# One group of gates in classical form behind the neighbourhood attention, features summed on VectorE, and modulation spread from global attention to w_out

## The chip, the cores and the metric

The kernel runs on one core of one Trainium2 chip. The core's engines run side by side, each with its own stream of instructions: TensorE (PE in the profile; PEld is its loading of stationary operands), VectorE (DVE), ScalarE (ACT), GpSimd (POOL) and SyncE (SP, which here only starts DMA transfers). The metric is the device time of one execution in microseconds, the median of several executions of one program.

## The reference

One encoder block on 512 tokens with a model width of 2048, all in float32:

```python
mod = silu(c) @ w_ada + b_ada                  # 2048 x 12288
sh1, sc1, g1, sh2, sc2, g2 = split(mod, 6)
h = rms_norm(x, norm1_w) * (1 + sc1) + sh1
qa, ka, va, qb, kb, vb, ga, gb = split(h @ w_in)
ya = global_gqa(rope(rms_norm(qa)), rope(rms_norm(ka)), va)     # 8 heads, 2 key-value heads
yb = neighbourhood_attention(qb, kb, vb, rpb)                   # 8 heads, windows of 8 x 16
m  = sigmoid(ga) * (ya @ w_oa) + sigmoid(gb) * (yb @ w_ob)
x  = x + g1 * (m @ w_out)
h2 = rms_norm(x, norm2_w) * (1 + sc2) + sh2
x  = x + g2 * ((silu(h2 @ w_gate) * (h2 @ w_up)) @ w_down)
out = rms_norm(x, final_w)
```

ga and gb are each 512 x 2048. Only sh1 and sc1 are needed at the start. The other four rows of mod (g1, sh2, sc2, g2) are first needed at the end of `w_out` and later: this is what the text calls modulation.

## The kernel before

**Float32 from two halves.** Every operand of a matmul is split into a high part (ScalarE, L167) and a low part (VectorE, L169), and each product is three matmuls: high by high, high by low, low by high (L187, L188, L189). A *unit* of weights is one 128x1024 block: one DMA of 0.5 MB on SP's queue into a buffer `raw`, one split on ScalarE and one on VectorE into `whl`, and then its products. There are four buffers `raw` and three `whl`, and one to three more in some stages.

**Classical and seven-product groups.** `form1` and `form2` compute a column group directly: a unit gives 24 products of 128x512 (a product being one of the three matmuls). `group7` computes 512 columns by seven half-size products in place of eight: VectorE first forms sums of weight blocks (`wforms`), and a group takes 336 matmuls of 128x256 where the classical form takes 192 of 128x512. The same trick needs sums of the features h: `whole_features` adds the high and low parts of a feature back together (L908, 16 additions of 128x512 on GpSimd), and `feature_forms` forms the sums from that (L918 to L921, VectorE) and splits them.

**The stages that the change touches, in order.** (1) The second half of the global queries, global attention, and the classical gates GA 12 to 15 and GB 0 to 3. (2) The groups by seven products: gates GB 4 to 15 in three groups (`gates7(1)` to `gates7(3)`) and the neighbourhood values in two. (3) Neighbourhood attention ("attention B"): four pairs of heads, each with classical queries and keys, then scores S, a softmax over ScalarE and VectorE, transposes into the bank T (L1008), and products into Y. (4) `w_oa`, (5) `w_ob`, both classical, with the gates, which were kept in DRAM, loaded again and multiplied in, and (6) `w_out`, classical, with the first residual. After these come the feed-forward groups, which the change leaves alone.

**Modulation as filler.** The late part of mod is 128 units. A unit is one DMA of 0.5 MB into a buffer `mw` (three of them, L351), and one VectorE operation of 128x1024 that multiplies it by a scalar of silu(c) and adds it to a sum `acc` (L373). 16 units make one group; then the sum is split, multiplied by a matrix of ones on TensorE (L390), copied out (L394) and kept in DRAM. `slot()` is called twice in each weight unit and once in each half of a head: it adds `pace["rate"]` to an account `due` and starts one step of modulation when the account has reached 1. `later` is a list of things to do, one per unit; `soon` holds what is due in some units' time. Before the change, 96 units run from the start of attention B through `w_oa` to the first five pairs of columns of `w_ob`, with their DMAs on GpSimd's queue, and 32 in `w_out`, with their DMAs on SP's queue. The loads of the residual's x and of the first gate's rows (`rows(gate, g1_d)`, on GpSimd's queue) are made through `later` in `w_out`'s first units. At the last pair of heads of attention B the eight results of global attention are loaded and split at once (`attended`).

**What sets the order.** The program is written stage by stage, and a scheduler of the framework then orders each engine's instructions by its own estimate of when operands are ready. So a step that is written behind another can come between its instructions, where its operands and buffers allow it. The tile pools set which buffers share memory: a pool that is released before another is allocated makes the second wait for the first.

## Time and profile before

| | |
|---|---|
| runs of the kernel | 2526.19, 2533.56, 2535.54 us (median 2533.56) |
| the profiled execution | 2529.71 us, of which the profile's span is 2527.9 us |
| mean granted clock of TensorE | 0.991 |
| TensorE busy | 2448.4 us, 97% of the span, 17327 matmuls |
| VectorE busy | 2022.3 us, 80% |
| ScalarE busy | 1073.6 us, 42% |
| GpSimd busy | 169.8 us, 7% |
| moved by DMA | 461.78 MB, mean 183 GB/s |

In the profiled execution the stages lie as follows, in microseconds from the start of the span. TensorE's first products of a stage and the last ones of the stage before can mix, so the bounds are those of its main part.

| stage | from | to |
|---|---|---|
| queries, global attention, gates GA 12 to 15 and GB 0 to 3 | 230 | 456 |
| groups by seven products | 456 | 640 |
| attention B | 640 | 859 |
| w_oa | 859 | 958.7 |
| w_ob | 958.7 | 1050.3 |
| w_out | 1050.3 | 1240 |

Rows of the profile read thus. A row of the view of windows gives, for a stretch of time, its length, then for each engine the busy time and, in brackets, the number of instructions; then the clock that TensorE was granted (1.00 is full speed), the share of time in which the DMA engines were busy, and what they moved. A row of waits gives an engine, its bank or tile and line, behind the arrow what it waited for, and then the total, the number of waits and the longest one. A row of a timeline gives an instruction's start and duration, and in square brackets the idle time ahead of it and what ended it.

### The profile page before, as it was taken

Reading aid. Unit: us, or ns where it says so; the run is one execution under the profiler, and the core shown is the slowest. Engines: PE = TensorE matmul, PEld = TensorE weight load, DVE = VectorE, ACT = ScalarE, POOL = GpSimd, SP = SyncE. Lnnn points to the kernel's source line nnn. Section 1 sums busy time; section 2 is a strip of 40 time slices with the busy share of each in tenths; the row PEclk is TensorE's granted clock in tenths of the full one; section 3 lists DMA queues with packets and bytes.
Section 4 is the critical chain, followed back from the end, with each engine's and each line's share of the span. In section 5 each row is a group of like instructions: output and inputs, shape, how many; then the busy total and the mean of one; then the engine's idle time right before and its main releaser. Section 6 shows DMA issues by size and latency. Waiting matters only on the chain.

```text
span 2527.9 us, 42439 instructions
## 1 busy us (share of the span) xinstructions
PE 2448.4 (97%) x17327; PEld 2285.7 (90%) x17327; DVE 2022.3 (80%) x2690; ACT 1073.6 (42%) x1470; POOL 169.8 (7%) x254
## 2 busy tenths in 40 slices
PE   8999998999999899999999999999999999999998
PEld 7888887999877678878999999999999998999997
DVE  8985877987688778558798888888888885778877
ACT  5223554444334433224764444444444454434333
POOL 0100002100012221002000000000000000000010
PEclk9999999999999999999999999999999999999999
DMA  9865232444687798588544434434444456647563
GB/s 352 312 230 164 61 102 74 130 130 142 209 269 264 263 317 281 167 303 294 164 126 134 134 119 138 129 110 134 127 132 134 127 162 225 205 142 250 186 236 129
DMA packets 213732, 461.78 MB, mean 183 GB/s; under 512 B 15152, under 2 KB 59552, under 8 KB 204832
## 3 DMA queue, kind: packets, MB, share of 16 engines
q1 hardware_dynamic: 176608, 318.68, 39.1%
q0 software_dynamic: 27424, 123.81, 14.1%
q10 hardware_dynamic: 9504, 16.58, 1.8%
q8 instruction: 136, 2.23, 0.4%
q14 instruction: 60, 0.49, 0.1%
HBM read 412.84 MB, written 46.17 MB: 182 GB/s over the span
## 4 chain that ended last, share of the span: by engine, by line
PE 65%; DVE 13%; issue 9%; DMA 9%; ACT 2%; POOL 1%; DVEq 0%; POOLq 0%; SPq 0%; ACTq 0%
PE mm L189 13%; PE mm L187 13%; PE mm L188 13%; PE S L187 5%; PE S L189 5%; PE S L188 5%; DMA mw<-in_ada_w 4%; DVE whl L169 3%; DMA raw<-in_w_down 3%; PE Y L187 2%; PE Y L188 2%; PE Y L189 2%; DVE raw L508 2%; DVE acc L373 1%; DMA yr<-y 1%
## 5 line engine op out<-in xcount | busy, mean ns | idle before, releaser
L167 ACT ACTIVATE whl<-raw 128x1024 fp32r<-128x1024 f32 (+1 forms) x483 | 453.6, 942 | 666.0 <-PE mm L189 253.5
L169 DVE TENSOR_TENSOR whl<-raw,whl 128x1024 fp32r<-128x1024 f32 (+1 forms) x483 | 519.7, 1087 | 133.4 <-ACT whl L167 132.8
L169 DVE TENSOR_TENSOR whl<-ta,whl 128x1024 fp32r<-128x1024 f32 x124 | 151.6, 1223 | 78.6 <-ACT whl L167 78.6
L167 ACT ACTIVATE whl<-tb 128x1024 fp32r<-128x1024 f32 x124 | 131.5, 1061 | 183.8 <-PE S L189 121.8
L167 ACT ACTIVATE whl<-ta 128x1024 fp32r<-128x1024 f32 x124 | 131.3, 1059 | 170.6 <-PE mm L189 110.6
L373 DVE SCALAR_TENSOR_TENSOR acc<-mw,cact,acc 128x1024 f32<-128x1024 f32 x124 | 158.6, 1279 | 37.6 <-DMA mw<-in_ada_w 36.8
L169 DVE TENSOR_TENSOR whl<-tb,whl 128x1024 fp32r<-128x1024 f32 x124 | 151.3, 1220 | 8.6 <-ACT whl L167 7.1
L679 DVE TENSOR_TENSOR ta<-raw,ta 128x512 f32<-128x512 f32 x124 | 86.4, 697 | 33.7 <-DMA raw<-in_w_down 27.8
L678 DVE TENSOR_TENSOR ta<-raw 128x512 f32<-128x512 f32 x124 | 85.5, 690 | 32.1 <-DMA raw<-in_w_down 29.5
L187 PE MATMUL mm<-x56h,whl 128*128 128x256 f32 x336 | 92.4, 275 | 0.0
L188 PE MATMUL mm<-x56l,whl 128*128 128x256 f32 x336 | 92.4, 275 | 0.0
L189 PE MATMUL mm<-x56h,whl 128*128 128x256 f32 x336 | 92.4, 275 | 0.0
L187 PE MATMUL mm<-whl,s 128*128 128x256 f32 x320 | 88.1, 275 | 0.0
L680 DVE TENSOR_TENSOR tb<-raw 128x512 f32<-128x512 f32 x124 | 86.3, 696 | 2.1 <-DMA raw<-in_w_down 0.2
L187 PE MATMUL mm<-x3h,whl 128*128 128x256 f32 x320 | 88.0, 275 | 0.0
L188 PE MATMUL mm<-x3l,whl 128*128 128x256 f32 x320 | 88.0, 275 | 0.0
L189 PE MATMUL mm<-x3h,whl 128*128 128x256 f32 x320 | 88.0, 275 | 0.0
L187 PE MATMUL S<-x56h,whl 128*128 128x256 f32 x320 | 88.0, 275 | 0.0
L188 PE MATMUL S<-x56l,whl 128*128 128x256 f32 x320 | 88.0, 275 | 0.0
L189 PE MATMUL S<-x56h,whl 128*128 128x256 f32 x320 | 88.0, 275 | 0.0
L188 PE MATMUL mm<-whl,s 128*128 128x256 f32 x320 | 88.0, 275 | 0.0
L189 PE MATMUL mm<-whl,s 128*128 128x256 f32 x320 | 88.0, 275 | 0.0
(1837 smaller groups left out, 8929.2 us busy)
## 6 DMA issues: line engine op xcount, KB each, us to landing
raw<-in_w_in SPq DMA_DIRECT2D x133, 512.0 KB, 4.5
mw<-in_ada_w POOLq DMA_DIRECT2D x96, 512.0 KB, 5.4
raw<-in_w_gate SPq DMA_DIRECT2D x92, 512.0 KB, 3.9
raw<-in_w_up SPq DMA_DIRECT2D x88, 512.0 KB, 3.8
raw<-in_w_down SPq DMA_DIRECT2D x88, 512.0 KB, 5.2
raw<-in_ada_w POOLq DMA_DIRECT2D x29, 1024.0 KB, 7.2
raw<-in_w_out SPq DMA_DIRECT2D x48, 512.0 KB, 5.5
mw<-in_ada_w SPq DMA_DIRECT2D x32, 512.0 KB, 4.8
```

Of the source, the lines that this page charges most:

```text
L167: high = pin(S.activation(hi, src, AF.Copy))
L169: latest[:] = [high, pin(eng.tensor_sub(lo, src, hi))]
L187: nc.tensor.matmul(o, lh, rh, start=start, stop=False, **kw)
L188: nc.tensor.matmul(o, lh, rl, start=False, stop=False, **kw)
L189: nc.tensor.matmul(o, ll, rh, start=False, stop=stop, **kw)
L373: behind(V.scalar_tensor_tensor(acc, part, cact[:, k:k + 1], acc, op0=ALU.mult, op1=ALU.add))
L508: V.scalar_tensor_tensor(raw, raw, 1.0, call, op0=ALU.mult, op1=ALU.mult, accum_out=y)
L678: V.tensor_sub(t1, b12, b11)
L679: V.tensor_sub(t2_, b22, t1)
L680: V.tensor_sub(t3, b22, b12)
```

## The change

- `slot()` caps its account at 1.5. A new `finish()` drains all units of modulation that are left up to the current limit, sets the rate to 0 and then does what is still due.
- Modulation's first group (16 units) runs from the second half of the global queries through global attention, at a rate of 0.45, in a pool of its own with one sum, and is drained behind the gates GA 12 to 15. 64 units run in attention B at 0.55, on through the moved gates and `w_oa`, and are drained behind `w_oa`. The last 48 run in `w_ob` at 0.7 and in `w_out` at 0.6 and then 0.35, and are drained ahead of the first half of the norm. Their DMAs go to GpSimd's queue up to the end of `w_ob`.
- The gates GB 4 to 7 are not computed by a group of seven products but classically, behind attention B. In that stretch the results of global attention are loaded, one in each unit; those of neighbourhood attention are loaded from the fourth unit of `w_oa`, through buffers `raw`.
- `whole_features` adds on VectorE and no longer on GpSimd.
- `w_ob` has no additional buffers any more (before: one `raw` and two `whl`).
- The load of the first gate's rows moves from ahead of the load of x's first quarter to ahead of its second.

```diff
--- before.py
+++ after.py
@@ -212,7 +212,7 @@
     pace = {"rate": 0.0, "due": 0.0}
 
     def slot():
-        pace["due"] += pace["rate"]
+        pace["due"] = min(pace["due"] + pace["rate"], 1.5)
         if pace["due"] >= 1 and (fetched or mod["next"] < mod["end"]):
             pace["due"] -= 1
             advance(mods)
@@ -226,6 +226,12 @@
             later.pop(0)()
         advance(bg)
         slot()
+
+    def finish():
+        while fetched or mod["next"] < mod["end"]:
+            advance(mods)
+        pace["rate"] = 0.0
+        flush()
 
     def flush():
         while bg or soon:
@@ -360,7 +366,7 @@
 
     def ada_acc(bias, done):
 
-        acc = mod["pool"].tile([P, 1024], F32, tag="acc", name="acc", bufs=2)
+        acc = mod["pool"].tile([P, 1024], F32, tag="acc", name="acc", bufs=mod["accs"])
         if bias is not None:
             G.memset(acc, 0.0)
             nc.gpsimd.dma_start(acc[0:1, :], b_ada[:, bias:bias + 1024])
@@ -826,6 +832,10 @@
     q = pair(p_a, "q", 4 * T, 1)
     bg.extend([normed(kv, 2, nw["k"], kT), normed(q_acc, 4, nw["q"], q), values()])
     q1 = [st(F32) for _ in range(NT)]
+    p_w = tc.alloc_tile_pool(name="p_w0", bufs=1, side="right")
+    mod.update(pool=p_w, end=16, accs=1)
+    mods.append(ada_mod(0, (s2, b_sc2, n2, t2, b_sh2)))
+    pace["rate"] = 0.45
     form2(w_in, QA + 512, hT, lambda i, b: S.activation(q1[i], b, AF.Copy))
     flush()
 
@@ -879,9 +889,10 @@
     q = pair(p_a, "q", 4 * T, 1)
     bg.append(normed(q1, 4, nw["q"], q))
     gates(sg_a, GA, 12, 16)
-    flush()
+    finish()
     for h in range(4):
         att_a(4 + h, q, h, 1)
+    p_w.release()
     p_a.release()
     p_q.release()
     p_o = []
@@ -905,7 +916,7 @@
         f = (p_o[0].tile([P, 2048], F32, tag="c", name="hc", bufs=1) if s != 1 else
              p_o[0].tile([P, 2048 + 64], F32, tag="whl", name="hw", bufs=1)[:, :2048])
         for k in range(4):
-            G.tensor_add(f[:, k * 512:(k + 1) * 512], *hT[4 * s + k])
+            V.tensor_add(f[:, k * 512:(k + 1) * 512], *hT[4 * s + k])
         whole.append(f)
 
     def feature_forms(s):
@@ -958,7 +969,7 @@
         group7(lambda s: wforms(w_in, 4 * s, VB + hh * 512), hs, range(4), lambda: d, by_tokens=True)
         nc.scalar.dma_start(v_d[hh], v)
 
-    for n in range(1, 4):
+    for n in range(2, 4):
         gates7(n)
     for hh in range(2):
         values7(hh)
@@ -967,8 +978,8 @@
     more_buffers(0, 0)
 
     p_w = tc.alloc_tile_pool(name="p_w", bufs=1, side="right")
-    mod.update(pool=p_w, end=96)
-    mods.extend(ada_mod(k, (s2, b_sc2, n2, t2, b_sh2)) for k in range(0, KT, 4))
+    mod.update(pool=p_w, end=80, accs=2)
+    mods.extend(ada_mod(k, (s2, b_sc2, n2, t2, b_sh2)) for k in range(4, KT, 4))
     g1_d, g2_d = ([dram.tile([1, 512], F32, name=f"g{n}d{q}") for q in range(4)] for n in (1, 2))
     mods.extend(ada_gate(c * D + q * 512, dst[q:]) for c, dst in ((2, g1_d), (5, g2_d)) for q in (0, 2))
     fetch()
@@ -1031,7 +1042,7 @@
         nc.sync.dma_start(yr, y_d[h])
         split(*hl, yr)
 
-    later.extend([lambda: None] * 4 + [lambda: pace.update(rate=0.85)])
+    later.extend([lambda: None] * 4 + [lambda: pace.update(rate=0.55)])
     for hp in range(4):
         hh, h0 = hp // 2, 2 * hp
         qs, ks = [pair(p_b, "q", T + 64, 3) for _ in range(2)], [pair(p_b, "k", T, 3) for _ in range(2)]
@@ -1044,20 +1055,17 @@
                 nc.sync.dma_start(vr.rearrange("p (i n) -> p i n", i=2), v_d[hh][:, i:i + 2])
                 for e in range(2):
                     split(*v[i + e], vr[:, e * 512:(e + 1) * 512])
-        if hp == 3:
-            p_h.release()
-            p_m = tc.alloc_tile_pool(name="p_m", bufs=1, side="left")
-            ya = [tuple(t[:, e * 512:(e + 1) * 512] for e in range(2))
-                  for t in (p_m.tile([P, 1024], F32R, tag=f"m{n}h", name=f"ya{n}", bufs=1) for n in range(8))]
-            for h in range(8):
-                attended(ya[h], h, raw_tile("yr")[:, :T])
         for j in range(2):
             att_b(h0 + j, qs[j], ks[j], v, slice((hp % 2 * 2 + j) * HD, (hp % 2 * 2 + j + 1) * HD))
 
     p_b.release()
+    p_y, p_ya = (tc.alloc_tile_pool(name=n, bufs=1, side="right", reuse_waits="tile") for n in ("p_y", "p_ya"))
+    yT, ya = ([pair(p, f"y{k}", T, 1) for k in range(8)] for p in (p_y, p_ya))
+    later.extend(lambda h=h: attended(ya[h], h, raw_tile("yr")[:, :T]) for h in range(8))
+    gates(sg_b, GB, 4, 8)
+    p_h.release()
+    p_m = tc.alloc_tile_pool(name="p_m", bufs=1, side="left")
     oa = [p_m.tile([P, 1024], F32, tag=f"m{j}l", name=f"oa{j}", bufs=1) for j in range(8)]
-    p_y = tc.alloc_tile_pool(name="p_y", bufs=1, side="right", reuse_waits="tile")
-    yT = [pair(p_y, f"y{k}", T, 1) for k in range(8)]
 
     class Tokens:
 
@@ -1078,17 +1086,17 @@
         return evac
 
     turn = itertools.cycle(("mm", "mm", "S"))
-    pace["rate"] = 0.72
-    later.extend([lambda: None] * 6 + [lambda h=h: attended(yT[h], 8 + h, p_y.tile([P, T], F32, tag="yr", name="yr", bufs=3))
-                                       for h in range(8)])
+    later.extend([lambda: None] * 3 + [lambda h=h: attended(yT[h], 8 + h, raw_tile("yr")[:, :T]) for h in range(8)])
     for j in range(0, KT, 2):
         tag = next(turn)
         form1([w_oa], j * P, 2, ya, [[bank(tag), bank(tag)]], gated(sg_a[j:], lambda e: oa[j // 2][:, e * 512:(e + 1) * 512]))
-    wq = p_y
-    more_buffers(1, 2)
+    finish()
+    p_ya.release()
+    p_w2 = tc.alloc_tile_pool(name="p_w2", bufs=1, side="left", reuse_waits="tile")
+    mod.update(pool=p_w2, end=128)
+    pace["rate"] = 0.7
     mx, mT = [], []
     for j in range(0, KT, 2):
-        pace["rate"] = 0.72 if j < 10 else 0.0
         o = [p_y.tile([P, T], F32, tag="o", name="o", bufs=4) for _ in range(2)]
         tag = next(turn)
         form1([w_ob], j * P, 2, yT, [[bank(tag), bank(tag)]], gated(sg_b[j:], lambda e: o[e]))
@@ -1103,7 +1111,6 @@
             else:
                 V.tensor_copy(mh, o3)
                 V.tensor_sub(ml, o3, mh)
-    wq = None
     p_y.release()
     p_w.release()
     aside.release()
@@ -1111,8 +1118,7 @@
     wq = tc.alloc_tile_pool(name="wq", bufs=1, side="right", reuse_waits="tile")
 
     x2_d = dram.tile([T, D], F32, name="x2d")
-    p_w = tc.alloc_tile_pool(name="p_w2", bufs=1, side="left", reuse_waits="tile")
-    mod.update(pool=p_w, queue=nc.sync, end=128)
+    mod["queue"] = nc.sync
     p_r = tc.alloc_tile_pool(name="p_r", bufs=1, side="right", reuse_waits="tile")
     gate = p_r.tile([P, D], F32, name="gate1")
     xc = {cc: p_r.tile([P, NT, 512], F32, tag=f"x{cc}", name=f"x{cc}") for cc in (3, 2)}
@@ -1123,12 +1129,12 @@
     x3d = xp.rearrange("(i p) d -> p i d", p=P)
 
     def load_x(cc):
-        if cc == 0:
-            rows(gate, g1_d)
         nc.sync.dma_start(xc[cc], x3d[:, :, cc * 512:(cc + 1) * 512])
 
     for cc in range(4):
-        later.extend([lambda: None] * (2 if cc == 0 else 3))
+        later.extend([lambda: None] * (2 if cc < 2 else 3))
+        if cc == 1:
+            later.append(lambda: rows(gate, g1_d))
         later.append(functools.partial(load_x, cc))
 
     def residual(cc, g, ssq, eng, x, keep=None):
@@ -1190,17 +1196,17 @@
     pace["rate"] = 0.6
     for cc in range(2):
         w_out_pass(cc, range(NT))
-    pace["rate"] = 0.5
+    pace["rate"] = 0.35
     for cc in (2, 3):
         w_out_pass(cc, (0, 1))
-    flush()
+    finish()
     norm((0, 1))
     bg.append(first_half())
     for cc in (2, 3):
         w_out_pass(cc, (2, 3))
     flush()
     norm((2, 3))
-    p_w.release()
+    p_w2.release()
 
 
 
```

The order of instructions on three engines shows what moves.

TensorE, the last heads of attention B (S is a bank of scores, from keys kh, kl and queries qh, ql; T takes the transposes of the softmax e; ya is global attention's result, the operand of `w_oa`; h0h, h0l, ... are features, the operands of the gates). Before:

```order
L188 MATMUL S<-kl,qh 128x256
L189 MATMUL S<-kh,ql 128x256
L187 MATMUL S<-kh,qh 128x256
L188 MATMUL S<-kl,qh 128x256
L189 MATMUL S<-kh,ql 128x256
L1008 MATMUL T<-ident,e 128x128 x4
L187 MATMUL mm<-ya_8042,whl 128x512
L188 MATMUL mm<-ya_8042,whl 128x512
```

Now, the same place:

```order
L189 MATMUL S<-kh,ql 128x256
L189 MATMUL mm<-h0h,whl 128x512
L187 MATMUL mm<-h1h,whl 128x512
L188 MATMUL mm<-h1l,whl 128x512
L189 MATMUL mm<-h1h,whl 128x512
L187 MATMUL mm<-h1h,whl 128x512
L188 MATMUL mm<-h1l,whl 128x512
L189 MATMUL mm<-h1h,whl 128x512
L187 MATMUL mm<-h2h,whl 128x512
L188 MATMUL mm<-h2l,whl 128x512
L189 MATMUL mm<-h2h,whl 128x512
L187 MATMUL mm<-h2h,whl 128x512
```

Before, the last two heads' 24 score products stand back to back and the transposes directly behind them; now the first of the moved gates' products stand between the scores and the transposes.

VectorE, behind global attention, at the features (hc and hw hold whole features, sa and sb their sums, s05 and s07 splits of these; `whl<-raw,whl` is the split of a weight unit of the gates GB 0 to 3). Before:

```order
L169 TENSOR_TENSOR ptl<-T,pth 128x4x128 x2
L169 TENSOR_TENSOR whl<-raw,whl 128x1024
L920 TENSOR_TENSOR sb<-hc 128x512
L918 TENSOR_TENSOR sa<-hc 128x512
L919 TENSOR_TENSOR sa<-sa,hc 128x512
L921 TENSOR_TENSOR sb<-hc,sa 128x512
L918 TENSOR_TENSOR sa<-hw 128x512
L169 TENSOR_TENSOR s05l<-sa,s05h 128x1024
```

Now:

```order
L169 TENSOR_TENSOR ptl<-T,pth 128x4x128 x2
L919 TENSOR_TENSOR hc<-h0h,h0l 128x512
L919 TENSOR_TENSOR hc<-h1h,h1l 128x512
L919 TENSOR_TENSOR hc<-h2h,h2l 128x512
L919 TENSOR_TENSOR hc<-h3h,h3l 128x512
L919 TENSOR_TENSOR hw<-h4h,h4l 128x512
L919 TENSOR_TENSOR hw<-h5h,h5l 128x512
L919 TENSOR_TENSOR hw<-h6h,h6l 128x512
L919 TENSOR_TENSOR hw<-h7h,h7l 128x512
L929 TENSOR_TENSOR sa<-hc 128x512
L931 TENSOR_TENSOR sb<-hc 128x512
L930 TENSOR_TENSOR sa<-sa,hc 128x512
```

The additions that GpSimd made now stand in VectorE's own stream, eight of them ahead of the first sum and of the next split of a weight unit.

SP's queue at the change from `w_ob` to `w_out` (raw is a weight unit, mw a unit of modulation, x0 and x1 quarters of x). Before:

```order
L1128 DMA x0_9655<-in_xp 128x4x512
L351 DMA mw_9692<-in_ada2_w 128x1024
L351 DMA mw_9710<-in_ada2_w 128x1024
L351 DMA mw_9730<-in_ada2_w 128x1024
L351 DMA mw_9748<-in_ada2_w 128x1024
L351 DMA mw_9785<-in_ada2_w 128x1024
L351 DMA mw_9817<-in_ada2_w 128x1024
L194 DMA raw_9819<-in_w_out 128x2x512
```

Now:

```order
L194 DMA raw_9749<-in_w_out 128x2x512
L1132 DMA x0_9497<-in_xp 128x4x512
L357 DMA mw_9540<-in_ada2_w 128x1024
L194 DMA raw_9645<-in_w_out 128x2x512
L357 DMA mw_9572<-in_ada2_w 128x1024
L357 DMA mw_9592<-in_ada2_w 128x1024
L357 DMA mw_9628<-in_ada2_w 128x1024
```

Before, the load of the fifth unit of `w_out` (raw_9819) stood behind six units of modulation and the first quarter of x; now that load (raw_9645) stands behind one unit of modulation and the quarter.

## The prediction, on record ahead of the run

> **What bounds the kernel now.** I read the engines' busy times first, then the changed stages as windows, then what TensorE waited for in them. The page says that TensorE sets the time:
>
> ```profile
> span 2527.9 us, 42439 instructions
> ...
> PE 2448.4 (97%) x17327; PEld 2285.7 (90%) x17327; DVE 2022.3 (80%) x2690; ACT 1073.6 (42%) x1470; POOL 169.8 (7%) x254
> ```
>
> Of the span it is idle for 2527.9 - 2448.4 = 79.5 us. So the change can gain only idle time of TensorE, products, or time at a lower clock. The stretches from global attention to `w_out`:
>
> ```profile
> 230.00:412.00 182.00, 178.83 (x971) 149.89 (x970) 134.98 (x302) 90.83 (x188) 0.00 (x0) 1.00 0.31 100
> 412.00:456.00 44.00, 33.50 (x161) 28.51 (x159) 37.88 (x33) 17.22 (x20) 26.28 (x16) 0.88 0.32 94
> ...
> 704.00:863.00 159.00, 137.51 (x682) 115.65 (x681) 127.66 (x179) 66.32 (x131) 32.61 (x58) 0.98 0.79 262
> 863.00:958.70 95.70, 90.88 (x423) 77.49 (x422) 76.88 (x93) 34.87 (x51) 21.59 (x38) 0.98 0.90 311
> 958.70:1050.30 91.60, 88.02 (x394) 75.90 (x393) 63.05 (x80) 24.79 (x31) 7.57 (x14) 0.96 0.65 221
> ...
> 1050.30:1205.00 154.70, 144.20 (x641) 123.55 (x640) 110.28 (x117) 53.79 (x74) 23.42 (x23) 0.96 0.81 279
> ```
>
> TensorE's idle time is the length less its busy time: 3.2 us before the features, 10.5 at them (412 to 456), 21.5 in the later part of attention B, 4.8 in `w_oa`, 3.6 in `w_ob`, 10.5 in `w_out`; together 54.1 of the 79.5 us. What it waited for, stretch by stretch (230 to 456, 704 to 840, 840 to 864, 864 to 1050, 1050 to 1206):
>
> ```profile
> PE mm L189 <- DVE whl L169: 9.0, 2, 6.8
> ...
> PE S L188 <- DVE kl L169: 4.4, 2, 3.5
> PE Y L390 <- DVE ada_o L394: 2.6, 1, 2.6
> PE Y L187 <- DVE ada_o L394: 1.5, 1, 1.5
> PE mm L189 <- DVE whl L169: 1.4, 1, 1.4
> ...
> PE T L1008 <- DVE e L1005: 5.9, 1, 5.9
> PE S L187 <- DVE sb L994: 2.9, 1, 2.9
> PE S L187 <- ACT kh L167: 1.4, 1, 1.4
> ...
> PE T L390 <- DVE accl L169: 2.1, 1, 2.1
> ...
> PE mm L187 <- ACT whl L167: 8.2, 1, 8.2
> PE T L390 <- DVE accl L169: 2.0, 2, 1.8
> ```
>
> Nearly all of it is VectorE late, or ScalarE. And some waits cost twice, since TensorE's clock stands at half in them and behind them:
>
> ```profile
> 429.90:440.20 10.30, 5.27 (x12) 4.20 (x13) 9.11 (x11) 4.64 (x5) 1.26 (x1) 0.50 0.22 58
> 856.60:863.40 6.80, 4.02 (x11) 2.84 (x12) 5.77 (x15) 6.69 (x17) 0.00 (x0) 0.50 0.66 223
> 924.80:928.30 3.50, 3.50 (x9) 2.78 (x10) 3.43 (x4) 2.49 (x4) 2.15 (x4) 0.51 0.82 262
> 1075.00:1085.30 10.30, 5.92 (x13) 4.31 (x14) 5.91 (x5) 3.17 (x3) 0.00 (x0) 0.50 0.91 320
> ```
>
> Half of the busy time in such a row is the loss: 2.6, 2.0, 1.7 and 3.0 us.
>
> **The change part by part**, against the profiled execution's 2529.7 us (span 2527.9 and 1.8 around it), which is 3.9 us under the median of the runs.
>
> *The classical group.* Two undisturbed stretches give a product's price:
>
> ```profile
> 550.00:600.00 50.00, 50.00 (x451) 50.00 (x450) 40.63 (x51) 23.23 (x25) 0.00 (x0) 1.00 0.45 131
> 1000.00:1050.00 50.00, 50.00 (x233) 43.73 (x232) 26.88 (x37) 13.47 (x17) 0.45 (x1) 1.00 0.48 158
> ```
>
> 50/451 = 0.111 us for one of the seven-product form, 50/233 = 0.215 us for a classical one. The group goes from 336 x 0.111 = 37.3 us to 192 x 0.215 = 41.2 us: **+3.9 us**, on the bounding engine, with nothing to hide it.
>
> *The tail of attention B.* The rows of 5.9, 2.9 and 1.4 us and the 2.0 us of half clock are its last heads, 12.2 us. TensorE's order before has 24 score products and then the transposes with nothing between; now products of the moved gates, which need only features and weights that come early, stand there, and 106 of them (23 us) still come behind the last head. **-11 us**; between -5, if the gates' own weight splits wait on VectorE behind the softmax (as the row of 1.4 us for `whl` shows once), and -12.2.
>
> The eight loads and splits of global attention's results, 0.69 us each on VectorE, go from one place at the last pair of heads to one in each of these units; they pass the weight loads on SP's queue and lie under 41 us of products. Without that cover the first products of `w_oa` would wait for the last load and split, some 3 us as a load of 0.5 MB takes below.
>
> *The rest of attention B.* The waits of 4.4, 2.6, 1.5 and 1.4 us, 9.9 together, are for VectorE's short operations for keys and for the sums' copies. In each stretch VectorE has 127.66/159 = 80% to do. A unit of modulation costs it
>
> ```profile
> L373 DVE SCALAR_TENSOR_TENSOR acc<-mw,cact,acc 128x1024 f32<-128x1024 f32 x124 | 158.6, 1279 | 37.6 <-DMA mw<-in_ada_w 36.8
> ```
>
> 1.28 us. By the order on VectorE 52 such operations lie before `w_oa` where 59 lay, and the stage is 41 us longer. I take half: **-5 us**, between 0 (the rests are latency) and -9.
>
> *w_oa and w_ob.* The modulation's share by stage:
>
> ```profile
> 863.00:958.70 95.70, 35.54 (x28) 15.03 (x28) 0.98 0.90 311
> 958.70:1050.30 91.60, 15.34 (x12) 4.84 (x9) 0.96 0.65 221
> ```
>
> In `w_oa` 15 are left by the order, so VectorE has 76.88 - 35.54 + 15 x 1.28 = 60.5 us to do in 95.7, and the losses of 4.8 and 1.7 us should mostly go; the drain behind it costs TensorE little while the next units' splits are done ahead. Eight loads of neighbourhood attention's results now take turns with the weights in the four `raw`, where they had buffers of their own; that is covered while weights run ahead, and a unit missed costs up to its 5 us. **-4 us** (-6.5 to +3). In `w_ob` there are 31 by the order, and VectorE has at most 63.05 - 15.34 + 31 x 1.28 = 87.4 us of 91.6: nearly full, with two `whl` and one `raw` fewer as cover. I take **+1 us** (-3 to +8).
>
> *w_out.* The wait of 8.2 us is for the fifth weight unit. SP's queue shows why:
>
> ```profile
> 1059.24 12.25 SPq L351 DMA_DIRECT2D mw<-in_ada_w  x6
> 1071.54 0.59 SPq L194 DMA_DIRECT2D raw<-in_w_out  x1
> ```
>
> Its load stands behind six loads of modulation, which wait for buffers that VectorE empties late. Now it stands behind one of these and x's quarter, and the first gate's rows no longer hold up GpSimd's queue ahead of it. But VectorE comes out of `w_ob` with modulation still to do, so that the split of this unit is some 3 us late. Of 8.2 + 2.0 + 3.0 = 13.2 us I take **-7 us** (-12 to -2); the drain ahead of the norm is in the smaller end.
>
> *The features.* VectorE's own operations take more than double while GpSimd adds:
>
> ```profile
> 410.32 0.69 DVE L169 TENSOR_TENSOR ptl<-T,pth 128x512 fp32r<-128x512 f32 x1 [1.38 <-ACT pth L167]
> ...
> 415.19 1.74 DVE L920 TENSOR_TENSOR sb<-hc 128x512 f32<-128x512 f32 x1 [2.53 <-POOL hc L908]
> ...
> 426.06 2.30 DVE L169 TENSOR_TENSOR s05l<-sa,s05h 128x1024 fp32r<-128x1024 f32 x1
> ...
> 432.52 1.22 DVE L169 TENSOR_TENSOR s07l<-sb,s07h 128x1024 fp32r<-128x1024 f32 x1
> ...
> 412.65 1.27 POOL L908 TENSOR_TENSOR hc<-h0h,h0l 128x512 f32<-128x512 f32 x1 [252.15 <-DVE whl L169]
> ```
>
> 0.69 us becomes 1.74, and 1.22 becomes 2.30. Of the eleven operations or so that ran beside GpSimd this is about 11 us, and waits for GpSimd's sums, as the 2.53 us here, are about 6 more. Against these 17 stand 16 additions of 0.69 = 11.0 us on VectorE. The chain to the first seven-product group is some 6 us shorter, and the loss of 10.5 + 2.6 = 13.1 us falls: **-6 us**, between -12 and +1 (eight additions now stand ahead of the next gate unit's split, 5.5 us where a unit of TensorE's work lasts 24 x 0.215 = 5.2 us and three buffers cover two such).
>
> The Trainium skill, Perfetto Trace Analysis, "Optimizing Scalar/DVE Operations", would offload a saturated VectorE's work to GpSimd, but warns that both share a read port, so that it might not help. Here VectorE is busy 37.88 of 44 us, so the advice speaks against this edit and the warning for it; by the advice alone the term would be about 0 and the sum 6 us higher; the doubled durations side with the warning.
>
> *Modulation in global attention.* 16 units of 1.28 us = 20.5 us on VectorE, which then has 155.5 of the 182 us before the features. DMA has room (share 0.31), and GpSimd's queue, which issues the loads, is idle there (0.00). Each can hold up a softmax step by at most its own 1.28 us; a third part of that for half of them is **+3 us** (0 to +10), the drain ahead of the last heads included.
>
> Sum: 3.9 - 11 - 5 - 4 + 1 - 7 - 6 + 3 = -25.1 us, so 2504.6 on the profiled execution's scale, and 3.9 more on the median's: **2508 us**.
>
> **The rivals.** *VectorE only moves its lateness.* The softmax steps' waits are latency and the moved gates' splits queue on VectorE behind them; the drains take what `w_oa` gains. For it: VectorE stays at 80% or above in most stages. Against: the 5.9 us wait has nothing on TensorE beside it, and now has. Half of the tail (-5), no gain in the rest and in `w_oa`, half in `w_out` (-3), features -3: 3.9 - 5 - 3 - 3 + 1 + 3 = -3 us, 2530: within 0.5% (12.7 us, about what a measurement of this kernel can tell from no change).
>
> *w_ob becomes bound by VectorE and modulation's loads* (slower). VectorE waited for the units' landing:
>
> ```profile
> DVE acc L373 <- DMA mw<-in_ada_w: 34.1, 28, 3.2
> ```
>
> 34.1/28 = 1.2 us each time. If each of the 31 operations in `w_ob` waits so, VectorE needs 87.4 + 37.2 = 124.6 us where TensorE needs 91.6: +33 us, and half clock behind repeated waits up to +10. With the rest of the sum (-26) that is 3.9 + 17 = 2550 on the median's scale, +0.7%. It decides from a mean wait of (91.6 - 87.4)/31 = 0.14 us on. Against it: the waits of before come where DMA's share is 0.79 to 0.90, and in `w_ob` it is 0.65; and with waits the account's cap lets units fall into `w_out`.
>
> These transfers go out on GpSimd's queue:
>
> ```profile
> mw<-in_ada_w POOLq DMA_DIRECT2D x96, 512.0 KB, 5.4
> ...
> mw<-in_ada_w SPq DMA_DIRECT2D x32, 512.0 KB, 4.8
> ```
>
> The landing takes 0.6 us longer than from SP's, which three buffers hide. The Trainium skill, SBUF — State Buffer, "SBUF: two separate sides", says that a transfer from GpSimd's queue can be starved while VectorE holds the port that both use; that would be this rival's cause, and the 0.6 us bears it out only a little.
>
> *The features gain nothing*, because 11.0 us more on VectorE in a stretch where it is 86% busy outweigh the faster operations: 2508 + 6 = 2514, or 2518 with half clock as before.
>
> **How the numbers follow.** The forecast has 0.66, the first rival 0.15, `w_ob` 0.07, the features 0.12. The forecast and the features' rival lie below 2520.9, but their upper ends do not: faster 0.76. The first rival and these ends give same 0.17, `w_ob` slower 0.07. For the range I take the favourable ends of about half the terms below (2484), and above it reaches to the first rival's 2530, less a little: 2528; out of it are `w_ob`, part of the first rival and a tail below.
>
> **What would show it.** Right: in attention B's last heads TensorE busy, with gate products between scores and transposes; VectorE's 128x512 operations at the features at 0.69 us throughout; the wait of 8.2 us at the fifth unit of `w_out` down to 3 or 4; `w_oa` without idle time or half clock; matmuls fewer by 144. Wrong: idle time of TensorE in `w_ob` with VectorE behind `mw`; new waits in global attention for e or pt beyond 5 us; a wait of more than 3 us at the drains behind `w_oa` or in `w_out`; VectorE late at the first seven-product sums as before.

## The result and the profile after

The changed kernel takes 2504.81 us (median of 4 runs, 2504.66 to 2507.35); the kernel before, in the same comparison, 2534.55 us (4 runs, 2526.19 to 2539.44). The ratio is 0.9888, with a 95% interval of 0.9861 to 0.9916: 1.1% faster. The forecast was 2508 us. Several of its terms were wrong, two of them by some 7 us, and the errors cancelled.

The profiled execution of the changed kernel took 2507.35 us, 2.5 above its median. The head of its page:

```profile
span 2505.6 us, 42099 instructions
...
PE 2452.3 (98%) x17183; PEld 2284.5 (91%) x17183; DVE 1992.1 (80%) x2675; ACT 1064.8 (42%) x1462; POOL 148.1 (6%) x247
```

TensorE has 144 matmuls fewer and is busy 3.9 us longer. That this equals the forecast price of the classical group is chance: busy time grows with half clock, and e2 below, with the same 17183 matmuls, is busy 2442.1 us. TensorE's idle time falls from 79.5 to 2505.6 - 2452.3 = 53.3 us. First one window of the kernel before, then those of the changed kernel, with three short ones behind global attention:

```profile
640.00:860.00 220.00, 198.76 (x999) 168.84 (x997) 164.31 (x231) 87.74 (x170) 38.61 (x69) 0.99 0.77 255
```

```profile
230.00:412.00 182.00, 175.06 (x916) 146.57 (x915) 146.83 (x308) 86.46 (x178) 11.12 (x20) 0.98 0.44 143
412.00:456.00 44.00, 40.90 (x212) 35.61 (x212) 39.63 (x61) 22.48 (x31) 0.00 (x0) 0.92 0.33 107
640.00:860.00 220.00, 214.76 (x1073) 181.46 (x1072) 155.46 (x229) 92.67 (x180) 30.73 (x55) 0.98 0.67 219
860.00:960.00 100.00, 96.49 (x440) 82.06 (x439) 65.98 (x78) 32.07 (x42) 16.10 (x28) 1.00 0.79 262
960.00:1050.00 90.00, 90.00 (x419) 78.74 (x418) 76.53 (x89) 27.82 (x34) 12.69 (x23) 1.00 0.79 271
...
424.00:434.00 10.00, 10.00 (x50) 8.80 (x49) 9.51 (x15) 6.79 (x8) 0.00 (x0) 1.00 0.31 110
434.00:444.00 10.00, 10.00 (x48) 8.76 (x47) 10.00 (x15) 3.88 (x5) 0.00 (x0) 1.00 0.31 98
444.00:454.00 10.00, 6.94 (x34) 6.25 (x33) 10.00 (x14) 5.59 (x7) 0.00 (x0) 0.77 0.30 97
```

From 640 to 860 us TensorE was idle for 21 us before and is now for 5; from 960 to 1050 it loses nothing, and its clock is full. From 860 to 960, most of which is `w_oa`, the clock is full too, but 3.5 us of idle time are left, where the prediction's signs of being right had none. But from 230 to 412 TensorE is idle for 6.9 us where it was 3.2, and in the three short windows VectorE has 29.5 of 30 us to do while TensorE, at the end, waits for the split of a weight unit.

TensorE's waits in the changed kernel, from 230 to 456, 640 to 860, and 960 to 1060 us:

```profile
PE T L804 <- issue: 2.9, 1, 2.9
PE mm L187 <- ACT whl L167: 2.5, 1, 2.5
PE Y L188 <- DVE ptl L169: 1.8, 1, 1.8
...
PE mm L187 <- ACT whl L167: 3.0, 1, 3.0
PE T L1019 <- ACT e L1011: 0.7, 2, 0.3
...
PE mm L187 <- ACT whl L167: 2.6, 1, 2.6
```

The row of 2.9 us lies ahead of global attention's heads; the kernel before has it too (2.0 us). The waits of 5.9 and 2.9 us in attention B's last heads are gone; one of 3.0 us for a gate's weights stands there now. The one of 8.2 us in `w_out` is 2.6.

The wait of 1.8 us for `ptl` comes from the drain of modulation. One of its steps on VectorE needs the finished sum back from DRAM, and VectorE stands still for it:

```profile
389.47 0.16 DVE L364 TENSOR_TENSOR t<-ada_c,vec 128x4 f32<-128x4 f32 x1 [2.15 <-DMA ada_c<-md]
```

Behind it in VectorE's stream stand a softmax step and the split of `ptl`, which starts at 390.15 us; TensorE goes on at 390.89, and at half clock from 391.4 us for 3.4 us. All five kernels here with modulation in global attention have this pair: VectorE idle for 2.0 to 2.3 us, TensorE for 1.7 to 2.0 us.

For comparing kernels I cut each trace at TensorE's first or last product of a kind: the first transpose of global attention's softmax (A), the 48th product with sums of features (B), the last such product (C), the first product of `w_out` (D), the first feed-forward product with sums (E), and the end. Microseconds, worked out from the start times of these products; the names are those of the experiments below.

| kernel | start to A | A to B: global attention, features | B to C: groups by seven | C to D: attention B, w_oa, w_ob | D to E: w_out and what follows | E to end | span |
|---|---|---|---|---|---|---|---|
| before | 295.2 | 164.8 | 178.2 | 412.1 | 236.7 | 1240.9 | 2527.9 |
| changed | 298.7 | 161.9 | 141.3 | 427.8 | 230.5 | 1245.4 | 2505.6 |
| e1 | 302.6 | 171.1 | 140.7 | 427.6 | 231.3 | 1243.1 | 2516.4 |
| e2 | 296.2 | 151.3 | 142.2 | 429.8 | 223.5 | 1246.4 | 2489.4 |
| e3 | 296.5 | 160.9 | 178.8 | 398.7 | 224.5 | 1239.6 | 2498.9 |
| e4 | 296.2 | 158.3 | 142.2 | 423.8 | 236.1 | 1244.9 | 2501.5 |
| e5 | 300.3 | 151.4 | 179.7 | 407.8 | 236.3 | 1240.0 | 2515.5 |
| e6 | 295.4 | 164.8 | 178.2 | 413.8 | 236.2 | 1239.5 | 2528.0 |
| e7 | 294.8 | 151.4 | 179.7 | 404.5 | 224.8 | 1241.5 | 2496.7 |
| e8 | 299.6 | 151.3 | 142.2 | 430.1 | 225.6 | 1242.2 | 2491.1 |
| e9 | 297.9 | 164.8 | 178.2 | 407.7 | 232.8 | 1241.5 | 2522.9 |
| e10 | 299.1 | 160.3 | 141.3 | 427.2 | 231.4 | 1238.8 | 2498.2 |

From before to changed: +3.5, -2.9, -36.9, +15.7, -6.2, +4.5, together -22.3 us, which is the difference of the spans. The change touches nothing in the last column, and in the first only by modulation's first seven units. Both move by some us from kernel to kernel, and so a single total says less than its stages. From A to B the kernels agree much better: 164.8 us in before, e6 and e9, and 151.3 or 151.4 in e2, e5, e7 and e8.

### The profile page after: what moved, and what is told of

It reads as the page before. It is cut to its first block, busy times and chain, and to the rows that moved or that the text cites. A ratio compares the mean times of both kernels' runs of the same rounds, so it can differ in the third digit from the quotient of the medians.

```text
span 2505.6 us, 42099 instructions
## 1 busy us (share of the span) xinstructions
PE 2452.3 (98%) x17183; PEld 2284.5 (91%) x17183; DVE 1992.1 (80%) x2675; ACT 1064.8 (42%) x1462; POOL 148.1 (6%) x247
## 4 chain that ended last, share of the span: by engine, by line
PE 62%; issue 16%; DVE 11%; DMA 6%; ACT 2%; POOL 1%; DVEq 0%; POOLq 0%; ACTq 0%; SPq 0%
PE mm L189 12%; PE mm L187 12%; PE mm L188 12%; PE S L189 5%; PE S L188 5%; PE S L187 5%; PE Y L188 2%; PE Y L187 2%; PE Y L189 2%; DVE whl L169 2%; DVE raw L514 2%; DMA raw<-in_w_down 2%; DMA mw<-in_ada_w 1%; DVE acc L379 1%; DMA g<-sga 1%
## 5 line engine op out<-in xcount | busy, mean ns | idle before, releaser
L684 DVE TENSOR_TENSOR ta<-raw 128x512 f32<-128x512 f32 x120 | 82.7, 689 | 40.1 <-DMA raw<-in_w_down 37.6
L357 POOL DMA_DIRECT2D mw<-in_ada_w x105 | 56.2, 536 | 708.1 <-DVE acc L379 299.2
```

The source lines that it names most:

```text
L357: mod["queue"].dma_start(w, ada2_w[n * P:(n + 1) * P, :])
L684: V.tensor_sub(t1, b12, b11)
```

## The experiments

Each ratio below is to the kernel before, run on the same chip in the same comparison.

**e1: features on GpSimd again.**

```diff
-            V.tensor_add(f[:, k * 512:(k + 1) * 512], *hT[4 * s + k])
+            G.tensor_add(f[:, k * 512:(k + 1) * 512], *hT[4 * s + k])
```

> The changed kernel (2504.8 us) with the 16 additions of whole_features back on GpSimd, all else as changed. Theory (VectorE's operations double beside GpSimd): about 6 us slower, 2511; VectorE's 128x512 operations at the features at 1.7 us again, and TensorE losing some 10 us ahead of the first seven-product group. Rival (the features gain nothing on VectorE, since 11 us of additions take the place of the doubled ones): within 2 us, 2503 to 2507.

2515.28 us, ratio 0.9942 (0.9922 to 0.9961): 10.5 us slower than the changed kernel by the medians, some 14 by the ratios. A to B is 9.2 us longer. The timeline of VectorE, first of e1 and then of the changed kernel:

```profile
429.64 1.75 DVE L931 TENSOR_TENSOR sb<-hc 128x512 f32<-128x512 f32 x1 [4.25 <-POOL hc L919]
432.56 1.75 DVE L929 TENSOR_TENSOR sa<-hc 128x512 f32<-128x512 f32 x1 [1.17 <-POOL hc L919]
...
442.20 2.29 DVE L169 TENSOR_TENSOR s05l<-sa,s05h 128x1024 fp32r<-128x1024 f32 x1
```

```profile
424.49 0.69 DVE L919 TENSOR_TENSOR hc<-h0h,h0l 128x512 f32<-128x512 f32 x1 [1.59 <-PE Y L189]
...
428.71 0.68 DVE L919 TENSOR_TENSOR hw<-h7h,h7l 128x512 f32<-128x512 f32 x1
429.32 0.68 DVE L929 TENSOR_TENSOR sa<-hc 128x512 f32<-128x512 f32 x1
...
432.86 1.22 DVE L169 TENSOR_TENSOR s05l<-sa,s05h 128x1024 fp32r<-128x1024 f32 x1
```

The first split of a feature sum, `s05l`, starts 15.5 us behind the start of attention's last product in e1 (426.7 us), and 8.7 us behind it in the changed kernel (424.2). Eight additions on VectorE start 0.60 us apart, so that they take 4.8 us and not 5.5. The rival falls; the theory had the size too small (6 us).

**e5: the same edit alone, on the kernel before** (G to V, the reverse of the diff above).

> The kernel before with one edit: the 16 additions of whole_features on VectorE. Theory (this edit is worth about 10 us by itself, as its undoing in the changed kernel cost): ratio to before 0.996, the stretch up to the first seven-product group about 10 us shorter, no operation of VectorE there doubled. Rival (it pays only together with modulation in global attention, which leaves VectorE late there): within 3 us of before.

2517.28 us, ratio 0.9944 (0.9929 to 0.9960), 12.5 us faster by the medians; A to B is 13.4 us shorter. The window in which TensorE lost 10.5 us and clock:

```profile
412.00:456.00 44.00, 43.40 (x266) 39.14 (x266) 41.46 (x58) 22.37 (x26) 0.00 (x0) 1.00 0.35 115
```

Idle time 0.6 us, clock 1.00: of the loss of 13.1 us, 0.6 is left. The stages that the edit does not touch add up to +1.0 us in this trace. The theory holds and its size too; the edit does not need the others.

**e2: no modulation in global attention.**

```diff
-    p_w = tc.alloc_tile_pool(name="p_w0", bufs=1, side="right")
-    mod.update(pool=p_w, end=16, accs=1)
-    mods.append(ada_mod(0, (s2, b_sc2, n2, t2, b_sh2)))
-    pace["rate"] = 0.45
...
-    finish()
+    flush()
...
-    p_w.release()
...
-    mods.extend(ada_mod(k, (s2, b_sc2, n2, t2, b_sh2)) for k in range(4, KT, 4))
+    mods.extend(ada_mod(k, (s2, b_sc2, n2, t2, b_sh2)) for k in range(0, KT, 4))
...
-    later.extend([lambda: None] * 4 + [lambda: pace.update(rate=0.55)])
+    later.extend([lambda: None] * 4 + [lambda: pace.update(rate=0.7)])
```

> The changed kernel without modulation in global attention: its 16 units go to attention B and w_oa (80 there, at a rate of 0.7). Theory (a small price in global attention, VectorE fuller in attention B): the stretch up to the features 3 us shorter, attention B and w_oa 2 to 5 us longer, 2504 to 2507 in all. Rival (modulation delays every softmax step in global attention, whose last products end 12 us later in the changed kernel's trace than before): 8 to 12 us faster up to the features, 2493 to 2498 in all.

2490.37 us, ratio 0.9835 (0.9813 to 0.9857): 14 us faster than the changed kernel, and by its median the fastest kernel of this study. A to B is 10.6 us shorter, C to D only 2.0 us longer, w_out 7.0 us shorter. The rival is right for the stretch up to the features; the gain in w_out was in neither account. Three further pairs, described below, price the modulation from A to B as well: e3 against e7 9.5 us, e4 against e8 7.0, e10 against e2 9.0. Where the 10.6 us lie is seen in e2's windows at the middle of global attention and at the features:

```profile
366.00:396.00 30.00, 30.00 (x177) 24.78 (x176) 22.39 (x56) 19.03 (x39) 0.00 (x0) 1.00 0.23 78
413.00:441.00 28.00, 28.00 (x143) 24.82 (x142) 28.00 (x39) 14.70 (x17) 0.00 (x0) 1.00 0.34 108
```

and in two of the changed kernel, the middle of global attention and its last heads (its windows at the features, 424 to 454 us, stand above):

```profile
366.00:396.00 30.00, 27.07 (x135) 22.23 (x134) 23.18 (x47) 15.47 (x29) 3.67 (x6) 0.94 0.37 116
396.00:424.00 28.00, 27.96 (x177) 22.86 (x176) 21.11 (x51) 15.11 (x33) 0.00 (x0) 1.00 0.23 68
```

At the features VectorE is full in both (28.00 of 28 us here, 29.5 of 30 in the changed kernel). Global attention's last product starts 117.1 us after A here and 125.5 us after A in the changed kernel, 8.4 us later, and everything that VectorE has to do for the features is later by as much. TensorE bridged part of that by taking gate products earlier: when attention ends, 102 classical products of the gates are left in the changed kernel, and 117 in e2 and in the kernel before. But these 15 products, 3.2 us, are then missing as cover for the features, and TensorE waits there. Between A and B TensorE is idle for 7.1 us in the changed kernel and for 1.3 in e2. Half clock (half of its busy time at a granted clock of 0.50) costs it 4.6 us and nothing. So idle time makes 5.8 of the 10.6 us and half clock 4.6. Half of the 16 units run between 349.8 and 375.8 us, with the drain, the sums' splits and copies and the reload behind them, where the clock also drops (0.94).

**e3: a group of seven products again.**

```diff
-    for n in range(2, 4):
+    for n in range(1, 4):
...
+        if hp == 3:
+            p_h.release()
+            p_m = tc.alloc_tile_pool(name="p_m", bufs=1, side="left")
+            ya = [...]
+            for h in range(8):
+                attended(ya[h], h, raw_tile("yr")[:, :T])
...
-    later.extend(lambda h=h: attended(ya[h], h, raw_tile("yr")[:, :T]) for h in range(8))
-    gates(sg_b, GB, 4, 8)
```

> The changed kernel with the gates GB 4 to 7 as a group of seven products again, and the results of global attention loaded and split at the last pair of heads as before; modulation, features and w_ob as changed. Theory (the moved gates cover the tail of attention B): the group gives back 3.9 us, the tail loses 10 to 12 us again, 2511 to 2513. Rival (attention B gained from the thinner modulation, not from the gates): 3.9 us faster, about 2501.

2501.37 us (2498.92 to 2510.18), ratio 0.9888 (0.9867 to 0.9908): no slower than the changed kernel, 3.4 us faster by the medians. By the totals the rival would be right. The stages say otherwise. TensorE's waits at the last heads in e3:

```profile
PE T L1019 <- DVE e L1016: 4.8, 2, 4.5
PE S L187 <- DVE sb L1005: 3.2, 1, 3.2
```

and the window around them:

```profile
825.00:865.00 40.00, 31.94 (x147) 27.14 (x146) 29.71 (x55) 19.30 (x37) 3.86 (x7) 0.83 0.53 170
```

The tail's waits are back, 8.1 us of idle time at a mean clock of 0.83. B to C and C to D together are 577.5 us in e3 and 569.1 in the changed kernel, 8.4 us more. What e3 wins lies elsewhere: 6.0 us in `w_out`, 5.8 us behind it, 2.2 us ahead of A, 1.0 us from A to B.

But not all of what e3 loses lies at the heads. It has another wait that the changed kernel does not have, at the drain of modulation behind `w_oa`:

```profile
PE Y L396 <- ACT acch L167: 5.8, 1, 5.8
```

Without the moved gates modulation has 8 weight units fewer to run beside, which is 16 calls of `slot()` or some 9 steps at its rate of 0.55, and in e3 9 of its operations stand on VectorE between 944 and 961 us, ahead of the sum that TensorE waits for. Idle time and half clock together cost e3 12.2 us at the last heads (825 to 865 us) and 8.4 at this wait; the changed kernel loses 7.0 at its last heads (815 to 840 us). So the moved gates seem to help in two ways, as cover for the heads and as room for modulation; no run parts the two. The pair was repeated without modulation in global attention.

**e7: e2 and e3 together** (rate 0.8 in attention B, where e2 has 0.7).

> The changed kernel with two edits undone: no modulation in global attention (80 units in attention B and w_oa, rate 0.8), and the gates GB 4 to 7 as a group of seven products again. Beside the run without modulation in global attention (2490.4 us) it shows the classical group a second time. Theory (the moved gates cover some 12 us of attention B's tail at a price of 3.9): 6 to 9 us slower than that run, 2496 to 2499. Rival (the group is worth nothing, as the medians of the first such pair say, 2504.8 and 2501.4): 2 to 5 us faster than that run, 2485 to 2488.

2499.52 us, ratio 0.9876 (0.9862 to 0.9890): 9.2 us slower than e2. B to D together are 584.2 us against 572.0, 12.2 us more, and the two waits are there again (4.7 and 2.4 us). `w_out` differs by 1.3 us here. The moved gates are worth some 8 to 12 us in their stages, as the theory says. In e3 and the changed kernel what lies behind hid it. That all of it is cover for the heads does not follow: there e7 loses 10.5 us and e2 2.4, and TensorE's waits for modulation's sums (L396) are 8.1 us in e7 and 1.6 in e2.

**e4: global attention's results through other buffers.**

```diff
-    later.extend(lambda h=h: attended(ya[h], h, raw_tile("yr")[:, :T]) for h in range(8))
+    later.extend(lambda h=h: attended(ya[h], h, io.tile([P, T], F32, tag="io", name="yr")) for h in range(8))
```

> The changed kernel with the eight results of global attention, loaded behind attention B, read through other buffers (io) in place of the weights' raw buffers. In the changed kernel's trace TensorE waits 3.0 us at 832 us for the split of a gate's weight unit, and stands at half clock behind it; no weight load is issued from 811 to 827 us. Theory (the loads hold the raw buffers until ScalarE has split them, which stands behind the last heads' copies, so weight loads stop): the wait goes, 5 to 7 us faster, 2498 to 2500. Rival (ScalarE's order or the queue itself is late, not the buffers): within 2 us, 2503 to 2507.

2503.88 us (2501.98 to 2505.06), ratio 0.9892 (0.9873 to 0.9912): within 1 us. The wait of 3.0 us becomes one of 1.9:

```profile
PE mm L189 <- DVE whl L169: 1.9, 1, 1.9
```

C to D is 4.0 us shorter and has no half clock, as the theory says; `w_out` is 5.6 us longer. **e8**, the same edit on e2:

> The changed kernel without modulation in global attention, and the eight results of global attention read through other buffers (io) in place of raw. Theory (the wait of 1.9 us at 817 us in the run without modulation in global attention, and the half clock behind it, come from weight loads that wait for raw buffers): 3 to 5 us faster than that run, 2485 to 2487. Rival (the io buffers make other work wait instead, in w_oa or before): within 2 us of it, 2488 to 2492.

2492.51 us (2485.36 to 2493.46), ratio 0.9845 (0.9830 to 0.9861), 2 us slower than e2 by the medians, with C to D the same (430.1 and 429.8) and a wait of 3.4 us for VectorE's split in place of 1.9 us for ScalarE's. Weight units are late there in either case; the buffers `raw` are not the whole cause.

**e6: only the gate's rows later, on the kernel before.**

```diff
-        if cc == 0:
-            rows(gate, g1_d)
...
-        later.extend([lambda: None] * (2 if cc == 0 else 3))
+        later.extend([lambda: None] * (2 if cc < 2 else 3))
+        if cc == 1:
+            later.append(lambda: rows(gate, g1_d))
```

> The kernel before with one edit: the load of the first gate's rows moved behind the load of x's first quarter, as in the change. Theory (these rows hold up GpSimd's queue, and with it modulation's next sum, whose buffers the loads ahead of the fifth unit of w_out wait for): the wait of 8.2 us and the half clock behind it go, 8 to 11 us faster. Rival (the fifth unit's load stands behind six loads of modulation on SP's queue in any case, and only a queue without these ahead of it helps): within 2 us of before, the wait stays.

2529.91 us, ratio 1.0000 (0.9986 to 1.0014). The wait stays:

```profile
PE mm L187 <- ACT whl L167: 8.4, 1, 8.4
```

**e9: only modulation's loads in w_out on GpSimd's queue, on the kernel before.**

```diff
-    mod.update(pool=p_w, queue=nc.sync, end=128)
+    mod.update(pool=p_w, end=128)
```

> The kernel before with one edit: modulation's 32 loads in w_out stay on GpSimd's queue, so that none stands ahead of the fifth weight unit's load on SP's. Theory (that place in SP's queue is the whole cause of the wait of 8.2 us): the wait and the half clock behind it go, 8 to 11 us faster. Rival (the load comes in time, but VectorE's split of it stands behind modulation, or GpSimd's queue is held up by the gate's rows and modulation only gets later): 0 to 3 us faster, and a wait of TensorE for VectorE's split or for x's quarter in its place.

2528.32 us, ratio 1.0002 (0.9988 to 1.0015). The wait for the fifth unit is gone, and another stands in its place:

```profile
PE mm L187 <- DVE ro L1139: 7.6, 2, 7.3
```

`ro` is VectorE's first step of the residual, which empties a bank. VectorE's timeline ahead of it:

```profile
1078.61 1.29 DVE L373 SCALAR_TENSOR_TENSOR acc<-mw,cact,acc 128x1024 f32<-128x1024 f32 x1 [4.01 <-DMA mw<-in_ada_w]
...
1086.64 1.28 DVE L373 SCALAR_TENSOR_TENSOR acc<-mw,cact,acc 128x1024 f32<-128x1024 f32 x1 [2.60 <-DMA mw<-in_ada_w]
...
1096.82 1.28 DVE L373 SCALAR_TENSOR_TENSOR acc<-mw,cact,acc 128x1024 f32<-128x1024 f32 x1 [1.46 <-DMA mw<-in_ada_w]
1098.02 0.68 DVE L1139 TENSOR_TENSOR ro<-mm,gate 128x512 f32<-128x512 f32 x1
```

`ro` stands behind units of modulation in VectorE's stream, and these now wait for their own loads. On GpSimd's queue, too, there are loads ahead of them: the last one of the gate's rows goes out there only at 1070.6 us, after a wait of 4.7 us, and the next of modulation's at 1071.3. The place in SP's queue was the cause of the first wait, but with modulation moved to another queue VectorE is late for the first banks instead.

**e10: the same edit on the changed kernel** (`mod["queue"] = nc.sync` left out).

> The changed kernel with modulation's loads in w_out on GpSimd's queue, as in the run before this one. In the changed kernel's trace TensorE waits 2.6 and 0.5 us for the fifth unit, half clock behind it. Theory (the one load of modulation ahead of it on SP's queue, and the memory's load by the others, make it late): w_out 4 to 7 us shorter, 2498 to 2501. Rival (VectorE comes late out of w_ob): within 2 us of 2504.8, the wait stays.

2503.60 us (2497.27 to 2512.85), ratio 0.9908 (0.9884 to 0.9931): no difference, and `w_out` takes 231.4 us (230.5). The wait stays:

```profile
PE mm L187 <- ACT whl L167: 4.0, 1, 4.0
```

So what is left of it in the changed kernel does not go with modulation ahead of it on SP's queue. The wait ends with the landing of the load, which ScalarE's split waits for, in the changed kernel and in e10:

```profile
1052.43 1.06 ACT L167 ACTIVATE whl<-raw 128x1024 fp32r<-128x1024 f32 x1 [5.51 <-DMA raw<-in_w_out]
```

```profile
1052.21 2.00 ACT L167 ACTIVATE whl<-raw 128x1024 fp32r<-128x1024 f32 x2 [12.17 <-DMA raw<-in_w_out]
```

This fifth load goes out at 1042.4 us in the changed kernel and lands 9.9 us later; in e10 it goes out earlier, at 1037.2 us, behind x's first quarter and no unit of modulation, and takes 14.9 us. The DMA engines' share is 0.98 from 1037.0 to 1052.4 us of the changed kernel. So the second half of e10's theory, the load on the memory by the others, is not refuted. Why the load goes out late, into the others, is seen in VectorE's timeline, first of the changed kernel, then of e2, behind the last gated product of `w_ob`:

```profile
1031.76 1.28 DVE L379 SCALAR_TENSOR_TENSOR acc<-mw,cact,acc 128x1024 f32<-128x1024 f32 x1
...
1033.29 1.28 DVE L379 SCALAR_TENSOR_TENSOR acc<-mw,cact,acc 128x1024 f32<-128x1024 f32 x1
...
1035.09 1.28 DVE L379 SCALAR_TENSOR_TENSOR acc<-mw,cact,acc 128x1024 f32<-128x1024 f32 x1
...
1036.62 1.22 DVE L169 TENSOR_TENSOR whl<-raw,whl 128x1024 fp32r<-128x1024 f32 x1
```

```profile
1022.16 1.29 DVE L1108 TENSOR_TENSOR m7l<-o,m7h 128x512 fp32r<-128x512 f32 x2
1023.37 2.35 DVE L169 TENSOR_TENSOR whl<-raw,whl 128x1024 fp32r<-128x1024 f32 x2
```

In the changed kernel three units of modulation stand ahead of the first weight split, 7.9 us behind VectorE's return to work at 1028.7 us; in e2 the splits come 4.3 us behind it (1019.0), the fifth unit's load goes out at 1020.1 us, ahead of all modulation in `w_out`, lands 5.8 us later, and TensorE waits for no weights in `w_out`. Both orders were made by the scheduler from the same lines; which of them comes out hangs on where modulation stands at that time. That VectorE's order is the cause is read from these timelines; no run changes it alone.

## Why the prediction was right, and where it was not

*The sum and the errors in it.* 2508 was forecast and 2504.8 measured; the total was right, partly by luck. "Features" was -6 and is -12.5 (e5; 13.4 us in the trace). "Modulation in global attention" was +3 and is +7.0 to +10.6 in the traces (e2 and the other three pairs). These two errors cancel so well that A to B is 2.9 us shorter where -3 was forecast. B to D was forecast at 3.9 - 11 - 5 - 4 + 1 = -15.1 us and is -21.2. Against that stand +3.5 us ahead of A and +4.5 us behind `w_out`, where the sum has nothing.

*Features: the mechanism right, the size too small.* The step that failed: 16 additions of 0.69 us counted nearly whole against the 17 us saved. In e5 TensorE loses 0.6 us in that window. The additions start 0.60 us apart, and in e5 28.2 us lie between attention's last product and the first product with a feature sum, in which VectorE gets its work done under the gate products that are left. The bound of -12 that I gave was about the value. The prediction's "more than double" holds for the 128x512 operations; the 128x1024 ones go from 1.22 to 2.30 us, 1.9 times. The Trainium skill, Perfetto Trace Analysis, "Optimizing Scalar/DVE Operations", says that offloading a saturated VectorE's work, even to GpSimd, may make sense, and warns that the two share a read port, so that it might not help; e1 and e5 side with the warning: the work on VectorE is worth 10.5 and 12.5 us.

*Modulation in global attention: the step that failed* is "each can hold up a softmax step by at most its own 1.28 us; a third part of that for half of them". I took VectorE's 155.5 of 182 us as room. The room is in the stretch's first part. At its end stands a chain that VectorE fills entirely, from the end of attention through the features to the first group by seven, so that what delays the heads delays all of it. Two things I left out altogether: the half clock behind the new waits (4.6 of the 10.6 us) and VectorE's idle wait for the drain's reload, ahead of a softmax step (2.15 us). I had also priced the two edits apart. With the additions on VectorE modulation costs 7.0 to 10.6 us from A to B; with them on GpSimd, e1 against the kernel before, it costs 6.3.

*The classical group and the tail:* +3.9 and -11, together -7.1. In their stages the moved gates are worth 8.4 us (e3) and 12.2 us (e7), 9.2 us by e7's medians. The price fits: the groups by seven take 36.9 us less (B to C), where 37.3 was forecast, and from C to D TensorE's busy time without the loss to half clock grows by 40.1, where 41.2 was. The cover for the heads is smaller than forecast. Idle time and half clock at the last heads fall from 12.7 us (840 to 864 us before) to 7.0, so -5.7 and not -11. The step that failed is that the gates' weights "come early": TensorE waits 3.0 us for one of them there, at half clock behind it. What the moved gates may give beside that, room for modulation, had no term. (The load of 0.5 MB put at "some 3 us" there takes 4.8 to 5.4 by the prediction's own rows; the sum does not use it.)

*The rest of attention B, w_oa, w_ob:* -5, -4 and +1, together -8. By idle time and half clock, too, the rest of attention B loses 1.6 us in place of 10.8, `w_oa` 3.5 in place of 6.5, and `w_ob` nothing in place of 6.4, together -18.6. With the group of seven kept, so that nothing but modulation's spread and the buffers differ there, C to D falls from 412.1 to 398.7 us (e3, -13.4); with 80 units in place of 64 and a rate of 0.8 to 404.5 (e7, -7.6). The term that was most wrong here is `w_ob`: the prediction left out its half clock before (5.62 us of busy time at 0.50 from 982.9 to 989.7 us, so 2.8 us) and reckoned with 31 units of modulation there by the order. The rival of a `w_ob` bound by VectorE and modulation's loads falls: `w_ob` runs from 945.6 to 1029.6 us, in which TensorE is never idle and VectorE does 18 units. The window that reaches 20 us into `w_out` has 22:

```profile
960.00:1050.00 90.00, 28.04 (x22) 10.14 (x19) 1.00 0.79 271
```

*w_out:* -7; D to E is 6.2 us shorter, and the wait at the fifth unit fell to 2.6 us where I wrote 3 or 4. I named SP's queue, the gate's rows and VectorE's lateness as causes. e6 shows that the rows alone gain nothing. e9 shows that SP's queue was the cause of the 8.2 us, and that a new wait of 7.3 us, for VectorE behind late modulation, takes the gain back. For what is left in the changed kernel, e10 shows that the place in SP's queue is not enough: the load then takes 14.9 us to land beside the others, against 5.8 in e2, where VectorE splits the first weights earlier and the load goes out ahead of modulation's. That is argued from the timelines, not tried by itself. Nor was it tried whether the rows and the queue together would do on the kernel before.

*Not foreseen:* the part behind `w_out` is 4.5 us longer in the changed kernel's trace, though its instructions stand in the same order on TensorE, VectorE and ScalarE as in e3, where it is 1239.6 us. The first difference is ScalarE's wait for a reload from DRAM, in the changed kernel and then in e3:

```profile
2132.56 1.06 ACT L167 ACTIVATE a<-ffr 128x1024 fp32r<-128x1024 f32 x1 [7.27 <-DMA ffr<-ffd]
```

```profile
2127.89 1.06 ACT L167 ACTIVATE a<-ffr 128x1024 fp32r<-128x1024 f32 x1 [3.65 <-DMA ffr<-ffd]
```

TensorE falls 2.2 us behind e3 there, and 3.7 us more in small waits for weight splits up to 2268 us. The load itself took about as long in both (6.3 us to landing); it was issued 3.9 us later, counted from E. E to end is 1242 to 1246 us in the changed kernel, e1, e2, e4 and e8, and 1239 to 1242 in all others, e10 with the moved gates among these. So it is not the moved gates as such; the cause stays open.

*Of the rivals,* "VectorE only moves its lateness" describes what happened between global attention's heads and the features, and in part at attention B's last heads; elsewhere most of the waits went. "The features gain nothing" is refuted by e5.

## What to carry to other kernels

Filler work on an engine is free only if that engine catches up before the next place where it is full: look for the stretch with 100% busy time behind the filler, not at the mean over the stage. Look also at what the filler's own drain waits for: a step that needs its result back from memory holds up everything behind it in that engine's stream. Price edits that load the same engine in neighbouring stages together. When a wait at a queue is removed, look at who else goes through the queue that takes the work over, and when an experiment's total is near the noise, cut the traces into stages before believing it.

## What the runs showed of the hardware beyond that

VectorE's additions of two 128x512 tiles take 0.69 us alone and 1.75 us beside GpSimd's additions, and its splits of 128x1024 1.22 and 2.29 us. The edit that only moves 16 additions from GpSimd, busy for 7% of the kernel, to VectorE, busy for 86% of that stretch, makes the kernel 12.5 us faster (e5). From E to the end TensorE, VectorE and ScalarE do the same instructions in the same order in all twelve kernels, and the traces differ by up to 7.6 us. Ahead of A they do so in the five kernels with modulation in global attention, and the traces differ by up to 6.4 us.
